# Retention: masked queries made by VectorE from the transposes' PSUM and a state without zero blocks; mLSTM's first masked queries issued first

## The chip, the cores and the metric

The kernel runs on one core of one Trainium2 chip. The metric is the device time of one execution in microseconds (us); the median of three runs counts.

## The reference, cut to what matters

A two-layer streaming encoder works on a prompt of 1024 frames and on eight streams of 16 frames, with a model width of 1024. Each layer normalises its input, multiplies it by one wide input projection, splits the result among four recurrent mixers (mLSTM, retention, SSD, HGRN2), gates each mixer's output, and brings the concatenation back through an output projection. The two mixers that matter here, per chunk of frames and per head (retention has four heads, with a query and key width of 64 and a value width of 128):

```python
# retention_block: carry S (k x v), fixed decay per head
s = einsum("lk,sk->ls", q, k) * dec
o = einsum("ls,sv->lv", s, v) + exp((idx + 1) * lg) * einsum("lk,kv->lv", q, s_prev)
s_new = exp(l * lg) * s_prev + einsum("sk,sv->kv", kw, v)
...
# mlstm_block: carry C (k x v), n, m
s = einsum("lk,sk->ls", q, k) * exp(d - m_t)
num = einsum("ls,sv->lv", s, v) + wi * einsum("lk,kv->lv", q, c_prev)
```

The SSD mixer begins with a causal convolution over four frames (`causal_dwconv`), whose first three input rows of the prompt are zero. All results are float32.

## The kernel before

The 1152 frames (1024 of the prompt, 128 of the eight streams) are nine chunks of 128; chunk 8 is the streams. **Projections** run on TensorE (PE) slab by slab, 256 columns of the weight matrix at a time (`slab_run`, L404 to L406 and L425 to L427). Each weight and activation is split into a high and a low part, so that a float32 product is three passes; ScalarE (ACT) makes the high part of the next slab and VectorE (DVE) or GpSimd (POOL) the low part (`slab_split`). An evacuation function `ev` takes each finished PSUM tile to SBUF.

**The order of the work** is written out by hand. A layer has ten units, `ORDER` = h0, r0, s0, m0, h1, r1, s1, m1, h2, h3 (h is HGRN2, r retention, s SSD, m mLSTM; each r, s and m unit has two heads or one group). `merge` lays the mixing of one unit, a generator `mix` of about 29 steps, between the projection matmuls of the next one: retention is mixed while SSD's projections run, mLSTM while HGRN2's run. So there are four retention units and four mLSTM units in the two layers. Every engine executes its own instructions strictly in the order in which this program issues them, and waits on semaphores for the others. SP issues the DMAs.

**Tiles** come from pools with a fixed number of slots: `t` (9 slots of 256 columns), `f` (18 of 384), `c` (21 of 516), and one PSUM pool of eight tiles for everything (`ps`). A new tile waits until a slot's last reader is done.

**Retention's mix** (L1018 to L1143) treats two heads at once: rows 0 to 63 of a transposed query tile are head 0, rows 64 to 127 head 1. `Z(c)` transposes queries and keys on PE (L1034), and ACT copies both to a `t` tile (L1036). `by_head` (L719) makes the masked ("padded") queries on POOL: two copies of the query tile, each multiplied by `self.HM`, which is 1 on one head's rows and 0 on the other's (L722, printed as the helper's line L212, `t<-t,cst`). `A(c)` multiplies keys by the masked queries (L1045, 256 columns for both heads) and DVE applies the causal mask. `B(c)` adds, in PSUM, the state's part (L1059: queries times `S`, 256 columns) and the scores' part (L1061), and updates the state: L1068, then one DVE addition per head and one scaling of all of `S` (L1077). `S` is 128 x 2 x 128: head 0's block has rows 0 to 63 of the first half, head 1's rows 64 to 127 of the second half, and the other two blocks are zero from a memset (L1020). `Cc(c)` transposes the normalised output (L1113). The steps go A(0); A(1), B(0); A(2), B(1), Cc(0); and so on. Masked queries of chunk c + 1 are asked for right behind A(c), the transposes of chunk c + 2 behind those:

```python
A(c)
if c + 1 < NCH:
    qz[c + 1] = self.by_head(qkT[c + 1][:, 0:128])
if c + 2 < NCH:
    Z(c + 2)
yield
```

**mLSTM's mix** (L770 to L970) has the same masked queries: its `Z(c)` calls `by_head` on the projected queries `q[g]`, and `A(c)` uses them in L833, behind a transpose of the keys (L832). Its first step begins with `load_e(0)`, `load_wi(0)` (DMAs), `use_wi(0)` (a DVE copy L205 `s<-f`, then a POOL product `f<-f,f`), `Z(0)`, `E(0)`.

**SSD's convolution** (`conv` in `unit_s`) copies each projected tile behind three columns of history into a `c` tile; for the first group of frames (g = 0) those three are set to zero by POOL (L1179). DVE then adds three taps (L1197), and SiLU follows on ACT and POOL. The convolution's results `post` and its SiLU's scratch are `f` tiles.

Of the kernel before, what the change touches and what calls it, by code (L numbers as in the profile page):

```python
# [48 lines left out]
NCH = 9  # L49
# [71 lines left out]
class Kernel:  # L121
    def __init__(self, nc, tc, ctx, T):
        self.nc, self.tc, self.T = nc, tc, T
        pool = lambda name, bufs, **k: ctx.enter_context(tc.tile_pool(name=name, bufs=bufs, **k))
        self.p_const = pool("const", 1)
        self.p_big = pool("big", 6)
        self.p_hi = pool("whi", 2)
        self.p_lo = pool("wlo", 2)
        self.p_raw = pool("wraw", 4)
        self.p_f = pool("f", 18)  # L130
        self.p_c = pool("c", 21)
        self.p_t = pool("t", 9)
        self.p_lay = pool("lay", 1)
        self.p_st = pool("st", 1)
        self.p_s = pool("s", 6)
        self.p_bl = pool("bl", 7)
        self.p_dram = pool("dram", 1, space=DRAM)
        self.p_tr = pool("tr", 8, space=PSUM)
        self.n = 0
        self.ticks = 0  # L140
        self.queue = []
        self.steps = 0
        self.after_queue = []
        self.rest = ((), 0)
# [586 lines left out]
    def unit_m(self, l, p):  # L731
# [38 lines left out]
        def mix():  # L770
# [156 lines left out]
            def Cc(c):  # L927
# [12 lines left out]
                if c == 8:  # L940
# [4 lines left out]
                    self.dma(T["o_s_n"][l, :, 2 * p:2 * p + 2].rearrange("n h k -> n (h k)"), nr[0:8])  # L945

            load_e(0)
            load_wi(0)
            use_wi(0)
            Z(0)  # L950
            E(0)
# [30 lines left out]
    def unit_r(self, l, p):  # L982
# [35 lines left out]
        def mix():  # L1018
            S = self.p_st.tile([128, 2, 128], F32, tag="st", name=self.nm("rS"))
            nc.gpsimd.memset(S, 0.0)  # L1020
            qkT, Pt, om, mx, stt, U, qz = {}, {}, {}, {}, {}, {}, {}
            gl = self.cst[:, C_GL:C_GL + 4]
# [6 lines left out]

            def Z(c):  # L1030
                j, i = divmod(c, 2)
                tr = self.ps("tr")
                for a in range(2):
                    nc.tensor.transpose(tr[:, 128 * a:128 * a + 128], qk[j][:, 256 * i + 128 * a:256 * i + 128 * a + 128], self.ident)  # L1034
                t = self.t(256)
                self.copy(t, tr[:, 0:256], "a")  # L1036
                qkT[c] = t
                if c == 8:
                    U["zq"] = [self.zq(t[:, 0:128], slice(64 * h, 64 * h + 64)) for h in range(2)]
                    U["km"] = self.km(qk[j][:, 256 * i + 128:256 * i + 256], "c")  # L1040

            def A(c):
                sc = self.ps("sc")[:, 0:256]
                w = self.t(256).rearrange("p (h t) -> p h t", h=2)
                nc.tensor.matmul(sc, qkT[c][:, 128:256], qz.pop(c), start=True, stop=True)  # L1045
                self.tt(w, sc.rearrange("p (h t) -> p h t", h=2), self.U[c == 8][:, None, :].to_broadcast([128, 2, 128]), ALU.mult)
                Pt[c] = w

            def B(c):
# [5 lines left out]
                if c == 8:  # L1055
                    po[1] = self.ps("sc")[:, 0:128]
                    zq = U.pop("zq")
                if 0 < c < 8:
                    nc.tensor.matmul(pb[:, 0:256], qt[:, 0:128], S.rearrange("p h e -> p (h e)"), start=True, stop=False)  # L1059
                for h in range(2):  # L1060
                    nc.tensor.matmul(po[h], w[:, h], v[j][:, i, h], start=(c in (0, 8)), stop=(c == 0 or (c < 8 and h == 1)))  # L1061
                if c == 8:
# [3 lines left out]
                if c < 8:  # L1066
# [3 lines left out]
                    for h in range(2):  # L1070
                        hs = slice(64 * h, 64 * h + 64)
                        new = tr[hs, 128 * h:128 * h + 128]
                        if c == 0:
                            self.copy(S[hs, h], new, "v")
                        else:
                            self.tt(S[hs, h], S[hs, h], new, ALU.add)
                    nc.vector.tensor_scalar(out=S, in0=S, scalar1=g_, scalar2=None, op0=ALU.mult)  # L1077
                    if c == 7:
                        for h in range(2):
                            self.dma(T["o_p_r"][l, 2 * p + h], S[64 * h:64 * h + 64, h])  # L1080
                else:
# [40 lines left out]
            yield  # L1122
            qz[0] = self.by_head(qkT[0][:, 0:128])
            Z(1)
            yield
            for c in range(NCH + 1):
                if c == 5:
                    load_states()
                if c < NCH:
                    A(c)  # L1130
                    if c + 1 < NCH:
                        qz[c + 1] = self.by_head(qkT[c + 1][:, 0:128])
                    if c + 2 < NCH:
# [14 lines left out]
    def unit_s(self, l, u):  # L1148
# [22 lines left out]
        def conv(a, g, ps):  # L1171
# [5 lines left out]
            e = "av"[(a + g) % 2]  # L1177
            if g == 0:
                nc.gpsimd.memset(t[:, 0:3], 0.0)  # L1179
            else:  # L1180
                self.copy(t[:, 0:3], pre.pop((a, g - 1))[:, 384:387], "v")
# [8 lines left out]
            cb = self.vA[:, 64 + 8 * l + ct:64 + 8 * l + ct + 1]  # L1190
            areas = [(o[:, 0:np_], lambda w: t[:, w:w + np_])]
            if g == 2:
                areas.append((o[:, 256:384].rearrange("p (n t) -> p n t", t=16), lambda w: sv[:, :, w:w + 16]))

            def taps(w):
                for oo, src in areas:
                    nc.vector.scalar_tensor_tensor(out=oo, in0=src(w), scalar=cw(w), in1=oo, op0=ALU.mult, op1=ALU.add)  # L1197

# [823 lines left out]
```

## Time and profile before

| what | us |
|---|---|
| median of three runs | 2413.29 |
| lowest and highest run | 2411.71, 2414.96 |
| the profiled execution | 2415.16 |
| its span, from the first to the last instruction | 2413.4 |

The profiled execution's own time is 1.8 us longer than its span, for what lies around the instructions. The profile lists each instruction with its line, its engine, the tiles that it writes and reads (`out<-in`), its start in us from the span's start, and the idle time of its engine before it with what ended that. PE is the matmul, PEld the weight load that overlaps it. A float32 product that isn't split beforehand appears as two MATMUL records, called passes here. Ends of matmuls are modelled, so the text takes times from start to start. PEclk is the granted TensorE clock as a share of 2.4 GHz.

### The profile page before, as it was taken

Reading aid. Unit: us, or ns where it says so; the run is one execution under the profiler, and the core shown is the slowest. Engines: PE = TensorE matmul, PEld = TensorE weight load, DVE = VectorE, ACT = ScalarE, POOL = GpSimd, SP = SyncE. Lnnn points to the kernel's source line nnn. Section 1 sums busy time; section 2 is a strip of 40 time slices with the busy share of each in tenths; the row PEclk is TensorE's granted clock in tenths of the full one; section 3 lists DMA queues with packets and bytes.
Section 4 is the critical chain, followed back from the end, with each engine's and each line's share of the span. In section 5 each row is a group of like instructions: output and inputs, shape, how many; then the busy total and the mean of one; then the engine's idle time right before and its main releaser. Section 6 shows DMA issues by size and latency. Waiting matters only on the chain.

```text
span 2413.4 us, 49607 instructions
## 1 busy us (share of the span) xinstructions
PE 2333.9 (97%) x18992; PEld 2258.8 (94%) x18992; DVE 1390.7 (58%) x3419; ACT 1076.4 (45%) x2780; POOL 976.2 (40%) x1179
## 2 busy tenths in 40 slices
PE   7999999999999998999989999999999999999998
PEld 7999999999999998899988999999899999888998
DVE  4756753773765376544368376537737654666443
ACT  6344563434455345433243445634344653454332
POOL 2443344353334335423135334432633452345353
PEclk9999999999999999999989999999999999999999
DMA  5111233221123222536411212323111333225552
GB/s 151 37 49 45 81 91 77 65 60 52 50 83 95 61 72 74 158 114 213 133 37 37 61 54 80 90 65 77 49 48 55 98 78 81 50 85 167 159 170 82
DMA packets 273736, 204.06 MB, mean 85 GB/s; under 512 B 57908, under 2 KB 264140, under 8 KB 273500
## 3 DMA queue, kind: packets, MB, share of 16 engines
q1 hardware_dynamic: 273180, 200.81, 29.2%
q8 instruction: 150, 2.46, 0.4%
q14 instruction: 86, 0.70, 0.1%
q0 software_dynamic: 320, 0.09, 0.0%
HBM read 148.53 MB, written 52.29 MB: 83 GB/s over the span
## 4 chain that ended last, share of the span: by engine, by line
PE 83%; DVE 8%; ACT 3%; issue 2%; DMA 1%; POOL 1%; SPq 1%; DVEq 0%; ACTq 0%; POOLq 0%
PE w L425 11%; PE w L404 11%; PE w L427 11%; PE w L426 11%; PE w L406 11%; PE w L405 11%; DVE f L212 3%; ACT f L215 2%; PE w L1310 1%; SPq L218 1%; DVE c L212 1%; PE w L1624 1%; PE w L1663 1%; PE w L1061 1%; PE w L833 1%
## 5 line engine op out<-in xcount | busy, mean ns | idle before, releaser
L425 PE MATMUL w<-hi,hnh 128*128 128x256 f32 (+1 forms) x2592 | 775.8, 299 | 0.0
L427 PE MATMUL w<-hi,hnl 128*128 128x256 f32 (+1 forms) x2592 | 731.9, 282 | 1.6 <-DVE hnl L492 1.6
L426 PE MATMUL w<-lo,hnh 128*128 128x256 f32 (+1 forms) x2592 | 731.7, 282 | 0.1
L425 PEld LDWEIGHTS w<-hi,hnh 128*128 128x128 f32 x2592 | 493.0, 190 | 6.1 <-issue 1.1
L426 PEld LDWEIGHTS w<-lo,hnh 128*128 128x128 f32 x2592 | 493.1, 190 | 3.5 <-issue 0.3
L427 PEld LDWEIGHTS w<-hi,hnl 128*128 128x128 f32 x2592 | 492.5, 190 | 2.2 <-DVE hnl L492 2.0
L215 ACT ACTIVATE f<-f 128x384 f32<-128x384 f32 (+1 forms) x475 | 244.1, 516 | 434.8 <-DVE f L212 275.0
L215 ACT ACTIVATE c<-c 128x512 f32<-128x512 f32 (+3 forms) x398 | 211.3, 534 | 292.4 <-DVE c L546 205.4
L212 POOL TENSOR_TENSOR f<-f,f 128x384 f32<-128x384 f32 (+2 forms) x268 | 226.7, 854 | 283.3 <-ACT f L215 210.3
L404 PE MATMUL w<-hnh,hi 128*128 128x384 f32 x960 | 339.3, 353 | 0.0
L212 POOL TENSOR_TENSOR lo<-raw,hi 128x512 fp32r<-128x512 f32 x148 | 195.0, 1318 | 332.3 <-ACT hi L202 279.2
L406 PE MATMUL w<-hnh,lo 128*128 128x384 f32 x960 | 324.6, 338 | 0.0
L405 PE MATMUL w<-hnl,hi 128*128 128x384 f32 x960 | 324.3, 338 | 0.0
L404 PE MATMUL w<-mxh,hi 128*128 128x384 f32 x768 | 268.7, 350 | 0.0
L406 PE MATMUL w<-mxh,lo 128*128 128x384 f32 x768 | 261.1, 340 | 0.0
L405 PE MATMUL w<-mxl,hi 128*128 128x384 f32 x768 | 260.9, 340 | 0.0
L212 POOL TENSOR_TENSOR c<-c,c 128x512 f32<-128x512 f32 (+2 forms) x120 | 128.9, 1083 | 221.2 <-ACT c L215 175.6
L212 DVE TENSOR_TENSOR lo<-raw,hi 128x512 fp32r<-128x512 f32 x140 | 114.4, 817 | 134.4 <-ACT hi L202 134.2
L404 PEld LDWEIGHTS w<-hnh,hi 128*128 128x128 f32 x960 | 181.6, 189 | 3.0 <-issue 1.8
L405 PEld LDWEIGHTS w<-hnl,hi 128*128 128x128 f32 x960 | 181.8, 189 | 0.8
L406 PEld LDWEIGHTS w<-hnh,lo 128*128 128x128 f32 x960 | 181.0, 189 | 0.0
L212 DVE TENSOR_TENSOR c<-c,w 128x384 f32<-128x384 f32 (+1 forms) x124 | 73.3, 595 | 184.8 <-PE w L406 121.6
(304 smaller groups left out, 3979.3 us busy)
## 6 DMA issues: line engine op xcount, KB each, us to landing
raw<-in_w_in SPq DMA_DIRECT2D x224, 128.0 KB
raw<-in_w_in SPq DMA_DIRECT2D x112, 256.0 KB
c<-mixd SPq DMA_DIRECT2D x96, 192.0 KB
raw<-in_w_out SPq DMA_DIRECT2D x64, 256.0 KB
xd<-c SPq DMA_DIRECT2D x66, 192.0 KB
mixd<-c SPq DMA_DIRECT2D x48, 256.0 KB
c<-xd SPq DMA_DIRECT2D x60, 192.0 KB
c<-sscr SPq DMA_DIRECT2D x36, 256.0 KB
```

Source lines behind the costliest of these rows:

```text
L212: (self.nc.vector if e == "v" else self.nc.gpsimd).tensor_tensor(out=out, in0=a, in1=b, op=op)
L215: self.nc.scalar.activation(out=out, in_=in_, func=func, scale=scale, bias=bias, **k)
L218: (e or self.nc.sync).dma_start(out=out, in_=in_)
L404: nc.tensor.matmul(o, hi[:, k, ms], xhi[:, k, :], start=(k == 0), stop=False)
L405: nc.tensor.matmul(o, hi[:, k, ms], xlo[:, k, :], start=False, stop=False)
L406: nc.tensor.matmul(o, lo[:, k, ms], xhi[:, k, :], start=False, stop=(k == KT - 1))
L425: nc.tensor.matmul(o, xhi[:, k, ts], hi[:, k, :w], start=(k == 0), stop=False)
L426: nc.tensor.matmul(o, xhi[:, k, ts], lo[:, k, :w], start=False, stop=False)
L427: nc.tensor.matmul(o, xlo[:, k, ts], hi[:, k, :w], start=False, stop=(k == KT - 1))
L833: nc.tensor.matmul(sc[:, 0:256], k[g][:, cs], qz.pop(c), start=True, stop=True)
L1061: nc.tensor.matmul(po[h], w[:, h], v[j][:, i, h], start=(c in (0, 8)), stop=(c == 0 or (c < 8 and h == 1)))
L1310: nc.tensor.matmul(po[:, 64 * h:64 * h + 64], pt[:, h], x_[:, 64 * h:64 * h + 64], start=True, stop=True)
```

## The change

Retention's `Z(c)` no longer copies the transposed queries: DVE multiplies them by `HM` straight out of PSUM into the first 256 columns of an `f` tile, and ACT copies the keys, 128 columns, into the last third of it. `by_head` is no longer called by retention; the masked queries of chunk c are thus made in `Z(c)`, which runs two chunks ahead. The state `S` becomes 128 x 128 with both heads' blocks stacked, without zero blocks and memset; `B(c)` multiplies each head's masked queries by all of `S`, two products of 128 columns instead of one of 256. The state's scaling has 128 columns instead of 256. The pool `t` has 8 slots instead of 9. mLSTM's first step calls `Z(0)` ahead of `load_e(0)`. The convolution's first group leaves its three history columns unset and starts each tap at the first column that has a frame behind it.

```diff
@@ -129,7 +129,7 @@
         self.p_raw = pool("wraw", 4)
         self.p_f = pool("f", 18)
         self.p_c = pool("c", 21)
-        self.p_t = pool("t", 9)
+        self.p_t = pool("t", 8)
         self.p_lay = pool("lay", 1)
         self.p_st = pool("st", 1)
         self.p_s = pool("s", 6)
@@ -944,10 +944,10 @@
                     self.copy(nr[0:8], tr[0:8, 0:128], "v")
                     self.dma(T["o_s_n"][l, :, 2 * p:2 * p + 2].rearrange("n h k -> n (h k)"), nr[0:8])
 
+            Z(0)
             load_e(0)
             load_wi(0)
             use_wi(0)
-            Z(0)
             E(0)
             yield
             for c in range(NCH + 1):
@@ -1016,9 +1016,8 @@
             G[c // 2] = z
 
         def mix():
-            S = self.p_st.tile([128, 2, 128], F32, tag="st", name=self.nm("rS"))
-            nc.gpsimd.memset(S, 0.0)
-            qkT, Pt, om, mx, stt, U, qz = {}, {}, {}, {}, {}, {}, {}
+            S = self.p_st.tile([128, 128], F32, tag="st", name=self.nm("rS"))
+            qkT, Pt, om, mx, stt, U = {}, {}, {}, {}, {}, {}
             gl = self.cst[:, C_GL:C_GL + 4]
 
             def load_states():
@@ -1028,21 +1027,24 @@
                     stt[j] = t
 
             def Z(c):
                 j, i = divmod(c, 2)
                 tr = self.ps("tr")
                 for a in range(2):
                     nc.tensor.transpose(tr[:, 128 * a:128 * a + 128], qk[j][:, 256 * i + 128 * a:256 * i + 128 * a + 128], self.ident)
-                t = self.t(256)
-                self.copy(t, tr[:, 0:256], "a")
+                t = self.f()
+                self.tt(t[:, 0:256].rearrange("p (h t) -> p h t", h=2), tr[:, None, 0:128].to_broadcast([128, 2, 128]),
+                        self.HM[:, :, None].to_broadcast([128, 2, 128]), ALU.mult)
+                self.copy(t[:, 256:384], tr[:, 128:256], "a")
                 qkT[c] = t
                 if c == 8:
-                    U["zq"] = [self.zq(t[:, 0:128], slice(64 * h, 64 * h + 64)) for h in range(2)]
+                    U["zq"] = [self.zq(t[:, 128 * h:128 * h + 128], slice(64 * h, 64 * h + 64)) for h in range(2)]
                     U["km"] = self.km(qk[j][:, 256 * i + 128:256 * i + 256], "c")
 
             def A(c):
                 sc = self.ps("sc")[:, 0:256]
                 w = self.t(256).rearrange("p (h t) -> p h t", h=2)
-                nc.tensor.matmul(sc, qkT[c][:, 128:256], qz.pop(c), start=True, stop=True)
+                nc.tensor.matmul(sc, qkT[c][:, 256:384], qkT[c][:, 0:256], start=True, stop=True)
                 self.tt(w, sc.rearrange("p (h t) -> p h t", h=2), self.U[c == 8][:, None, :].to_broadcast([128, 2, 128]), ALU.mult)
                 Pt[c] = w
 
@@ -1055,10 +1057,10 @@
                 if c == 8:
                     po[1] = self.ps("sc")[:, 0:128]
                     zq = U.pop("zq")
-                if 0 < c < 8:
-                    nc.tensor.matmul(pb[:, 0:256], qt[:, 0:128], S.rearrange("p h e -> p (h e)"), start=True, stop=False)
                 for h in range(2):
-                    nc.tensor.matmul(po[h], w[:, h], v[j][:, i, h], start=(c in (0, 8)), stop=(c == 0 or (c < 8 and h == 1)))
+                    if 0 < c < 8:
+                        nc.tensor.matmul(po[h], qt[:, 128 * h:128 * h + 128], S, start=True, stop=False)
+                    nc.tensor.matmul(po[h], w[:, h], v[j][:, i, h], start=(c in (0, 8)), stop=(c < 8))
                 if c == 8:
                     for h in range(2):
                         self.streams_in(po[h], zq[h], lambda n: stt[n // 4][:, n % 4], False)
@@ -1071,13 +1073,13 @@
                         hs = slice(64 * h, 64 * h + 64)
                         new = tr[hs, 128 * h:128 * h + 128]
                         if c == 0:
-                            self.copy(S[hs, h], new, "v")
+                            self.copy(S[hs], new, "v")
                         else:
-                            self.tt(S[hs, h], S[hs, h], new, ALU.add)
+                            self.tt(S[hs], S[hs], new, ALU.add)
                     nc.vector.tensor_scalar(out=S, in0=S, scalar1=g_, scalar2=None, op0=ALU.mult)
                     if c == 7:
                         for h in range(2):
-                            self.dma(T["o_p_r"][l, 2 * p + h], S[64 * h:64 * h + 64, h])
+                            self.dma(T["o_p_r"][l, 2 * p + h], S[64 * h:64 * h + 64])
                 else:
                     g_ = gl[:, 2 + p:3 + p]
                     km = U.pop("km")
@@ -1120,7 +1122,6 @@
 
             Z(0)
             yield
-            qz[0] = self.by_head(qkT[0][:, 0:128])
             Z(1)
             yield
             for c in range(NCH + 1):
@@ -1128,8 +1129,6 @@
                     load_states()
                 if c < NCH:
                     A(c)
-                    if c + 1 < NCH:
-                        qz[c + 1] = self.by_head(qkT[c + 1][:, 0:128])
                     if c + 2 < NCH:
                         Z(c + 2)
                     yield
@@ -1175,9 +1174,7 @@
             t = self.c(411)
             pre[a, g] = t
             e = "av"[(a + g) % 2]
-            if g == 0:
-                nc.gpsimd.memset(t[:, 0:3], 0.0)
-            else:
+            if g > 0:
                 self.copy(t[:, 0:3], pre.pop((a, g - 1))[:, 384:387], "v")
             np_ = G3 if g < 2 else 256
             self.copy(t[:, 3:3 + np_], ps[:, 0:np_], e)
@@ -1188,13 +1185,15 @@
             o = self.f()
             cw = lambda w: self.vA[:, 32 * l + 8 * w + ct:32 * l + 8 * w + ct + 1]
             cb = self.vA[:, 64 + 8 * l + ct:64 + 8 * l + ct + 1]
-            areas = [(o[:, 0:np_], lambda w: t[:, w:w + np_])]
+            areas = [((lambda w: o[:, 0:np_]), lambda w: t[:, w:w + np_])]
+            if g == 0:
+                areas = [((lambda w: o[:, 3 - w:np_]), lambda w: t[:, 3:w + np_])]
             if g == 2:
-                areas.append((o[:, 256:384].rearrange("p (n t) -> p n t", t=16), lambda w: sv[:, :, w:w + 16]))
+                areas.append(((lambda w: o[:, 256:384].rearrange("p (n t) -> p n t", t=16)), lambda w: sv[:, :, w:w + 16]))
 
             def taps(w):
                 for oo, src in areas:
-                    nc.vector.scalar_tensor_tensor(out=oo, in0=src(w), scalar=cw(w), in1=oo, op0=ALU.mult, op1=ALU.add)
+                    nc.vector.scalar_tensor_tensor(out=oo(w), in0=src(w), scalar=cw(w), in1=oo(w), op0=ALU.mult, op1=ALU.add)
 
             def silu():
                 s = self.f()
```

## Rows read from the trace of the kernel before

**Rows 1.** The page's head and its part 1, busy us (share) and instructions per engine.

```profile
span 2413.4 us, 49607 instructions
...
PE 2333.9 (97%) x18992; PEld 2258.8 (94%) x18992; DVE 1390.7 (58%) x3419; ACT 1076.4 (45%) x2780; POOL 976.2 (40%) x1179
```

**Rows 2.** Waits of PE, whole span: who <- releaser: us in total, times, longest.

```profile
PE w L1045 <- POOL c L1179: 7.9, 4, 2.0
...
PE w L833 <- POOL t L212: 3.7, 4, 0.9
```

**Rows 3.** Timeline of PE, first unit: start, us, engine, line, operation, tiles, shape, [idle <-releaser].

```profile
196.09 0.34 PE L406 MATMUL w<-hnh,lo 128*128 128x384 f32 x1
...
196.70 0.38 PE L1034 MATMUL w<-cst,c 128*128 128x128 f32 x2
```

**Rows 4.** Timeline of PE, second retention unit, around A(1).

```profile
600.89 0.34 PE L406 MATMUL w<-hnh,lo 128*128 128x384 f32 x1
...
603.19 0.70 PE L1045 MATMUL w<-t,t 128*128 128x256 f32 x2 [1.96 <-POOL c L1179]
603.72 0.38 PE L1034 MATMUL w<-cst,c 128*128 128x128 f32 x2
```

**Rows 5.** Timeline of POOL, second retention unit, before A(1).

```profile
601.57 0.99 POOL L212 TENSOR_TENSOR f<-f,f 128x384 f32<-128x384 f32 x1 [3.21 <-ACT f L215]
602.52 0.61 POOL L212 TENSOR_TENSOR t<-t,cst 128x256 f32<-128x256 f32 x1
```

**Rows 6.** Windows of equal work around A(1): length, busy per engine, PEclk, DMA, GB/s.

```profile
199.88:206.95 7.07, 5.10 (x21) 4.05 (x21) 2.87 (x6) 2.31 (x6) 2.59 (x4) 0.76 0.15 37
600.89:606.41 5.52, 3.56 (x21) 2.87 (x21) 2.86 (x6) 2.31 (x6) 2.58 (x4) 1.00 0.20 48
1391.81:1397.35 5.54, 3.57 (x21) 2.88 (x21) 2.87 (x6) 2.33 (x6) 2.59 (x4) 1.00 0.28 71
1793.58:1800.59 7.01, 5.05 (x22) 4.14 (x21) 3.11 (x6) 2.30 (x6) 2.58 (x4) 0.76 0.14 37
```

**Rows 7.** Timeline of DVE, first retention unit, around Z(0) and Z(1).

```profile
189.73 0.42 DVE L546 TENSOR_SCALAR c<-w 128x256 f32<-128x256 f32 x1 [2.48 <-PE w L427]
195.59 0.62 DVE L1197 SCALAR_TENSOR_TENSOR f<-c,vA,f 128x384 f32<-128x384 f32 x1 [5.44 <-ACT f L215]
```

**Rows 8.** Groups of DVE by form, whole span: count | busy us, mean ns | idle.

```profile
L212 DVE TENSOR_TENSOR t<-w,cst 128x256 f32<-128x256 f32 x36 | 14.9, 414 | 3.8 <-PE w L1045 3.8
```

**Rows 9.** Timeline of PE, first mLSTM unit, around A(0) and A(1).

```profile
420.62 0.28 PE L427 MATMUL w<-hi,hnl 128*128 128x256 f32 x1
...
421.94 0.70 PE L833 MATMUL w<-t,f 128*128 128x256 f32 x2 [0.93 <-POOL t L212]
...
422.60 0.28 PE L426 MATMUL w<-lo,hnh 128*128 128x256 f32 x1
...
423.77 0.29 PE L427 MATMUL w<-hi,hnl 128*128 128x256 f32 x1
...
424.56 0.28 PE L426 MATMUL w<-lo,hnh 128*128 128x256 f32 x1
```

**Rows 10.** Timeline of POOL, first mLSTM unit, before A(0).

```profile
420.23 1.04 POOL L212 TENSOR_TENSOR f<-f,f 128x384 f32<-128x384 f32 x1 [10.61 <-DVE s L205]
421.23 1.80 POOL L212 TENSOR_TENSOR t<-f,cst 128x256 f32<-128x256 f32 x3
```

**Rows 11.** Timeline of ACT: the first mLSTM unit's first query tile.

```profile
398.65 0.49 ACT L202 ACTIVATE f<-w 128x384 f32<-128x384 f32 x1 [2.37 <-PE w L406]
```

**Rows 12.** Timeline of PE, first retention unit, B(1): state's part, scores' part, update.

```profile
215.50 0.59 PE L1059 MATMUL w<-rS,t 128*128 128x256 f32 x2
215.93 0.61 PE L1061 MATMUL w<-c,t 128*128 128x128 f32 x4
216.38 0.60 PE L1068 MATMUL w<-c,c 128*128 128x256 f32 x2
```

**Rows 13.** Waits of DVE, whole span: us in total, times, longest.

```profile
DVE lo L212 <- ACT hi L202: 134.2, 70, 5.1
```

## The prediction, made before the change ran

> **What bounds the kernel now.** First the page's head and its busy times [rows 1]: TensorE (PE) is busy 97% of the span, VectorE (DVE) 58%, ScalarE (ACT) 45%, GpSimd (POOL) 40%. The reader should see that work on the other three engines costs time only where PE waits for it, and that only 2413.4 - 2333.9 = 79.5 us of the span is left in which PE does nothing. So the second view is the list of PE's own waits [rows 2]. Two of its entries are at lines that the change touches: L1045, the score product of retention's A(c), four times 7.9 us in all, and L833, the same product of mLSTM, four times 3.7 us. Both are put down to POOL. Four is the number of retention units and of mLSTM units (two per layer), so each unit pays once. The third view is the timeline, to see what each of these waits costs from one matmul's start to a later one's.
>
> **Retention's wait.** It falls on the second chunk. In A(0) PE goes from the last projection pass before the scores to the transposes behind them in 196.70 - 196.09 = 0.61 us [rows 3]. In A(1), here of the second unit, the same way takes 603.72 - 600.89 = 2.83 us, with 1.96 us of idle time in it [rows 4]. The wait costs 2.22 us. POOL's own timeline tells why [rows 5]: the masked copy of the queries (L722, `t<-t,cst`) stands behind a product of the convolution's SiLU, and that product waited 3.21 us for ACT. The copy then runs from 602.52, and PE starts as it ends. (The wait's label names POOL's next instruction, the memset of L1179.) So PE waits neither for data nor for POOL's throughput, but for the order of POOL's queue.
>
> The four units do the same work behind this wait, so equal stretches can be laid beside each other [rows 6]: 7.07, 5.52, 5.54 and 7.01 us. In the first and the fourth the mean granted clock is 0.76, not 1.00: after the pause PE spent about half of the stretch at 1.2 GHz and only then went back to 2.4 GHz. That costs 1.55 and 1.47 us more. The four waits together: 4 x 2.22 + 1.55 + 1.47 = 11.9 us.
>
> With the change Z(c) makes the masked queries on DVE out of the transposes' PSUM, two chunks ahead, and A(c) waits for DVE and for an ACT copy half as wide. Would these be in time for A(0) and A(1)? DVE's timeline of the first unit [rows 7] has a clamp ending at 190.15, and then nothing for 5.44 us until the convolution's taps begin at 195.59. Z(0) and Z(1) are issued in that gap (PE's steps are some 3 us apart), each needing one product. For its length I take that of DVE's existing 128x256 product out of PSUM with a broadcast constant, 0.414 us [rows 8]; POOL's copy at 0.61 [rows 5] is the other end. Even at 0.61 both are done before 195.59, while A(0) comes at 196.3 and A(1) would come at 200.1. The waits go whole: **-11.9 us**. The new wait, of DVE for the transposes, has the taps queued behind it and behind those the SiLU on ACT and POOL; but A(c)'s mask, just ahead in DVE's queue, waits for the matmul ahead of those transposes anyway, so it adds at most the transposes themselves, two passes of 128 columns at some 0.11 us [rows 12]. What is late next in A(1) would be the PSUM tile of the scores; no row shows PE waiting for one in this stage.
>
> **mLSTM's wait.** It falls on A(0). PE needs 422.60 - 420.62 = 1.98 us from the last projection pass before it to the second pass behind it; in A(1) the same way takes 424.56 - 423.77 = 0.79 us [rows 9]. The wait costs 1.19 us (its idle time is 0.93; the first passes after it are slower). On POOL, `use_wi(0)`'s product started at 420.23, after 10.61 us of idleness that a DVE copy ended; the masked copy is behind it, from 421.23 [rows 10]. Asked for first, the copy needs only q[0]. ACT wrote the first group of the queries at 398.65 [rows 11], and POOL was idle for 10.61 us. So it is made long before PE asks. Behind it in POOL's queue is only `use_wi(0)`, which still starts when DVE lets it, at 420.23, and ends at 421.23; Z(1) then ends about 421.9, and A(1), moved to some 422.8, finds it ready. Z issues no DMA, so SP's queue keeps its order. **4 x 1.19 = -4.8 us.**
>
> **PE's added work.** The state loses its zero blocks, so for chunks 1 to 7 of four units one product of 256 columns becomes two of 128, each with its own weight load: 28 times. Every such product is two passes. Two passes of 256 take 215.93 - 215.50 = 0.43 us, four passes of 128 with four loads 216.38 - 215.93 = 0.45 us [rows 12]. **28 x 0.02 = +0.6 us.** These passes have the shape of the new ones and load as often, so I take no wider bound. The Trainium skill, "TensorE: Matmul & The Clock Gate", section "LDWEIGHTS (loading the stationary operand)", prices a load of 128 columns at about 107 ns, which speaks against the change: the 56 added loads, if nothing hid them, would cost an estimated 6.0 us, and the sum would be -10.7 instead of -16.1. The trace doesn't agree: a pass of 128 takes 0.11 us with its load in it.
>
> **What costs nothing, and under which cover.** DVE gets 36 products, 36 x 0.414 = 14.9 us, 3.7 per unit. Their cover is DVE's 42% of idle time; if it is gone, PE waits for PSUM evacuations. POOL loses 36 masked copies, 16 memsets of the convolution and four of the state; ACT's copies and DVE's scaling of the state halve. Nobody on PE's path waits for these after the first chunks: 0. The first tap columns of the convolution become up to 3 of 384 narrower: 0. The tiles of Z move from the pool t to f (18 tiles; the convolution of x keeps six through this stage, Z needs four), and t goes from nine to eight. No row shows a wait for a t slot on PE. Between nothing and one more wait of mLSTM's size per mLSTM unit, 4.8 us, I take nothing, since t loses its largest user.
>
> **Sum.** -11.9 - 4.8 + 0.6 = -16.1 us. The profiled execution took 2415.16 us (span 2413.4), 1.9 above the median of the runs; it becomes 2399.1, and the median 2413.29 - 16.1 = **2397.2 us**.
>
> **Rivals.**
> (a) The slow clock isn't part of what is saved. It followed two of four equal pauses [rows 6], so in another execution it may follow none: then 4 x 2.22 + 4.8 - 0.6 = 13.1 us go, 2400.2. The Trainium skill, same page, "What's actually happening", has the clock's watch running freely, so that the slow stretch varies between runs; two of four here agrees. Chance 0.12.
> (b) One wait finds a successor. If mLSTM's A(0) then waits as long for its own transposes, -11.9 + 0.6 leaves 2402.0 (chance 0.08). If it is retention's A(1), for a PSUM tile or DVE, -4.8 + 0.6 leaves 2409.1 (chance 0.05). Against both: the rows of DVE and POOL show the producers idle at the time [rows 7, 10].
> (c) Nothing is gained: PE comes early and gives it all back at its next wait on another engine, +0.6, 2413.9. For it: 68 us of waiting remain elsewhere. Against: what those engines do is started by PE's own evacuations and so moves with PE. Chance 0.05.
> (d) Slower: DVE becomes PE's bound. DVE is in order, and in this stage it also splits weights, waiting for ACT's half: 134.2 us in 70 waits, 1.92 each, 5.1 the longest [rows 13]. A Z product behind such a wait holds its PSUM tile. With two DVE splits for each of three slabs, 24 in the four units, all passed on whole to PE: 24 x 1.92 = 46 us, less 16.1, 2443. It decides once DVE comes back later than PE needs one of its eight PSUM tiles. Against: PE doesn't wait for DVE's other evacuations behind the same waits today. Chance 0.04.
> The forecast keeps 0.66.
>
> **Numbers.** About 0.2% (4.8 us) is what a measurement can tell from no change; the bound of faster is 2408.5. Faster: 0.66 + 0.12 + 0.08 = 0.86; same: the second half of (b) and (c), 0.10; slower 0.04. The range takes in the forecast, (a) and the first half of (b), 0.86 together, and the bound of the t slots, 2397.2 + 4.8 = 2402.0. The three runs spread by 3.3 us, so I add that on both sides: 2393.9 to 2405.3, rounded to 2393.5 and 2405.5.
>
> **What would show it.** Right: L1045 and L833 are gone from PE's waits, or below 0.3 us; DVE has 36 products `f<-w,cst` near 0.41 us, POOL no `t<-t,cst`; the state's product (L1059 before) has 112 passes of 128 columns about 0.11 us apart; PE's idle time is about 68 us; no slow clock follows A(1). Wrong: L1045 still waits, now for DVE; or PE waits in the same stages for a tile that DVE should have emptied; or PE's idle time shrinks as forecast and the time doesn't.

## The result and the profile after

| | median, us | runs | lowest to highest |
|---|---|---|---|
| before | 2413.44 | 4 | 2411.71 to 2414.96 |
| changed | 2398.77 | 4 | 2394.35 to 2400.93 |

The ratio is 0.9937 (95% interval 0.992 to 0.9954): faster by 14.7 us where 16.1 were forecast. Run again beside the experiments below, the changed kernel took 2397.25 us. The profiled execution took 2394.35 us with a span of 2392.3; it is the lowest of the four, and the end of this section says what that adds to the difference of the two profiles.

Page, head and part 1, changed kernel (busy us, share, instructions):

```profile
span 2392.3 us, 49680 instructions
...
PE 2324.5 (97%) x19048; PEld 2254.5 (94%) x19048; DVE 1391.3 (58%) x3455; ACT 1073.8 (45%) x2780; POOL 950.5 (40%) x1123
```

Against [rows 1] PE's idle time fell from 79.5 to 2392.3 - 2324.5 = 67.8 us. DVE's busy time hardly grew in this profile, although DVE took over 36 products of 14.9 us; in the profile of the changed kernel run again it was 1395.6 us. What that rests on is told below. PE's waits, changed kernel (who <- releaser: us in total, times, longest):

```profile
PE w L1604 <- DVE f L212: 10.8, 8, 2.4
PE w L269 <- DMA t<-in_hgrn_norm_w: 9.1, 1, 9.1
PE w L1691 <- DVE f L1682: 7.7, 3, 3.1
PE w L510 <- DVE f L212: 7.4, 2, 4.0
PE w L1584 <- POOL f L212: 6.9, 4, 3.2
PE w L1572 <- POOL f L212: 5.0, 5, 1.2
```

Both entries of [rows 2] are gone: A(c)'s score product is now L1047, mLSTM's is still L833, and neither is in the list, which goes on down to waits of 0.2 us. What leads it lies outside the stages touched. PE's timeline, changed kernel, at A(1) of the second retention unit (compare [rows 4]):

```profile
593.59 0.34 PE L406 MATMUL w<-hnh,lo 128*128 128x384 f32 x1
593.76 0.59 PE L1047 MATMUL w<-f 128*128 128x256 f32 x2
594.19 0.38 PE L1034 MATMUL w<-cst,c 128*128 128x128 f32 x2
```

From the last projection pass to the transposes it is 0.60 us now, as in A(0) before [rows 3], where it was 2.83. Windows of the changed kernel over the same passes as [rows 6] (length, busy of PE, PEld, DVE, ACT, POOL, PEclk, DMA share, GB/s):

```profile
197.53:200.84 3.31, 3.31 (x21) 2.93 (x21) 1.48 (x4) 1.81 (x5) 1.01 (x1) 1.00 0.00 0
593.59:596.88 3.29, 3.29 (x22) 2.92 (x21) 1.46 (x4) 1.79 (x5) 1.02 (x1) 1.00 0.00 0
1380.66:1383.95 3.29, 3.29 (x21) 2.92 (x21) 1.47 (x4) 1.80 (x5) 1.02 (x1) 1.00 0.01 2
1779.33:1782.62 3.29, 3.29 (x21) 2.91 (x21) 1.46 (x4) 1.81 (x5) 1.01 (x1) 1.00 0.00 0
```

PE is busy in all of each window and the granted clock is 1.00 in all four. The windows are 3.76, 2.23, 2.25 and 3.72 us shorter, 12.0 together. DVE's timeline, changed kernel, around Z(0) and Z(1) of the first unit (compare [rows 7]):

```profile
188.10 0.42 DVE L212 TENSOR_TENSOR f<-w,cst 128x256 f32<-128x256 f32 x1 [0.32 <-PE w L1034]
190.96 0.42 DVE L212 TENSOR_TENSOR f<-w,cst 128x256 f32<-128x256 f32 x1 [2.44 <-PE w L1034]
193.15 2.90 DVE L1196 SCALAR_TENSOR_TENSOR f<-c,vA,f 128x381 f32<-128x381 f32 x3 [1.76 <-ACT f L215]
```

Both products are done 6 us before A(1) asks at 197.71. mLSTM's first unit, changed kernel, PE and POOL timelines (compare [rows 9, 10]):

```profile
414.59 0.27 PE L832 MATMUL w<-cst,f 128*128 128x128 f32 x1
414.70 0.60 PE L833 MATMUL w<-t,f 128*128 128x256 f32 x2
```

```profile
414.08 1.04 POOL L212 TENSOR_TENSOR f<-f,f 128x384 f32<-128x384 f32 x1 [10.04 <-DVE s L205]
415.08 1.23 POOL L212 TENSOR_TENSOR t<-f,cst 128x256 f32<-128x256 f32 x2
```

`use_wi(0)`'s product (414.08) still waits some 10 us for DVE, but A(0)'s masked queries no longer stand behind it: L833 starts at 414.70 without idle time, while POOL is still in that product.

**Where the rest of the profiled difference is.** Laying each projection pass of the two profiled executions beside the same pass of the other, the changed kernel's lead grows in the touched stages in eight steps, 3.75, 1.18, 2.22, 1.18, 2.23, 1.19, 3.71 and 1.21 us, 16.7 in all. The two executions differ by 20.8 us; the remaining 4 come from stretches that the change doesn't touch, at the start and near 2195 us, where one execution had the lower clock and the other not. The medians' differences (14.7 us and, run again, 16.5) lie near the 16.7, not near the 20.8.

### The profile page after: what moved, and what is told of

Its sections match the earlier page's. It is cut to its first block, busy times and chain, and to the rows that moved or that the text cites. A ratio compares the mean times of both kernels' runs of the same rounds, so it can differ in the third digit from the quotient of the medians.

```text
span 2392.3 us, 49680 instructions
## 1 busy us (share of the span) xinstructions
PE 2324.5 (97%) x19048; PEld 2254.5 (94%) x19048; DVE 1391.3 (58%) x3455; ACT 1073.8 (45%) x2780; POOL 950.5 (40%) x1123
## 4 chain that ended last, share of the span: by engine, by line
PE 86%; DVE 8%; ACT 3%; issue 1%; POOL 1%; DMA 1%; SPq 0%; DVEq 0%; ACTq 0%; POOLq 0%
PE w L404 12%; PE w L405 11%; PE w L406 11%; PE w L425 11%; PE w L427 11%; PE w L426 11%; DVE f L212 3%; ACT f L215 2%; PE w L1309 1%; DVE c L212 1%; PE w L1572 1%; PE w L1662 1%; PE w L1623 1%; PE w L1063 1%; PE w L489 1%
```

## The experiments

| kernel | median, us (runs) | before, us | ratio [95%] |
|---|---|---|---|
| mLSTM's reordering alone | 2407.99 (11) | 2413.93 | 0.9977 [0.9968, 0.9985] |
| lead of two chunks, still on POOL | 2402.48 (5) | 2413.93 | 0.9955 [0.9942, 0.9968] |
| on DVE, one chunk ahead | 2401.84 (5) | 2413.93 | 0.9959 [0.9947, 0.9971] |
| convolution's part alone | 2416.35 (12) | 2413.93 | 1.0009 [1.0, 1.0019] |
| changed kernel again | 2397.25 (6) | 2413.72 | 0.9934 [0.992, 0.9947] |
| compact state alone | 2417.54 (12) | 2413.72 | 1.0016 [1.0007, 1.0026] |
| changed, 3 more DVE products from PSUM | 2425.29 (6) | 2413.72 | 1.0048 [1.0034, 1.0063] |
| changed, HGRN2's keys two steps earlier | 2405.52 (6) | 2413.72 | 0.9965 [0.9951, 0.9978] |
| changed, 3 more DVE products in SBUF | 2408.76 (7) | 2413.99 | 0.9975 [0.9964, 0.9985] |
| changed, HGRN2's keys asked for one step later | 2402.6 (5) | 2413.99 | 0.9953 [0.9939, 0.9966] |
| changed, 1 more DVE product in SBUF | 2396.67 (5) | 2414.18 | 0.9935 [0.9922, 0.9949] |

**The parts one by one.** The kernel before with mLSTM's part only:

```diff
+            Z(0)
             load_e(0)
             load_wi(0)
             use_wi(0)
-            Z(0)
```

> The kernel before with one edit: mLSTM's first step issues its masked queries ahead of the loads. Theory (PE waits for places in POOL's queue): L833 no longer waits for POOL, four times 1.19 us from start to start, so 4.8 us less than the kernel before, ratio 0.998; the four waits of L1045 stay at 7.9 us. Rival (the gain of the change is retention's alone, and mLSTM's first scores then wait as long for their own transposes or a PSUM tile): L833 waits for another engine instead, within 1 us of the kernel before.

It gained 5.9 us. L833's wait is gone, L1045's stands at 7.9 us as before, and the stretch of passes around A(0), 4.49, 4.75, 4.49 and 4.77 us before, is 3.31, 3.57, 3.31 and 3.56: 4.75 in all. That is the term of 4.8.

The kernel before with only the lead (a full-sized state, POOL still the maker):

```diff
 def Z(c):
     ...
+    qz[c] = self.by_head_f(t[:, 0:128])
...
-            qz[0] = self.by_head(qkT[0][:, 0:128])
...
-                    if c + 1 < NCH:
-                        qz[c + 1] = self.by_head(qkT[c + 1][:, 0:128])
```

> The kernel before with one edit: retention's masked queries are asked for two chunks ahead, right behind the transposes' copy, but still made by POOL (into a wider tile pool, so that no slot is short); state, convolution and mLSTM as before. Theory (the order of POOL's queue): the product for chunk 1 now stands ahead of the convolution's SiLU product, L1045's wait is gone, 8.9 us less (four pauses of 2.22) and up to 12 where slow-clock stretches go with them; ratio 0.995 to 0.9965. Rival (POOL is the wrong engine, only DVE with PSUM at hand is quick enough): L1045 still waits for POOL, 6 us or more in total, and the time is within 3 us of the kernel before.

And only the other engine (DVE makes the masked queries from SBUF, one chunk ahead as before):

```diff
-            qz[0] = self.by_head(qkT[0][:, 0:128])
+            qz[0] = self.by_head_v(qkT[0][:, 0:128])
...
-                        qz[c + 1] = self.by_head(qkT[c + 1][:, 0:128])
+                        qz[c + 1] = self.by_head_v(qkT[c + 1][:, 0:128])
```

> The kernel before with one edit: retention's masked queries are made by DVE instead of POOL, but as late as before, one chunk ahead and out of SBUF; state, convolution and mLSTM as before. Theory (the wait comes from POOL's queue standing behind ACT): on DVE the product for chunk 1 stands behind the mask of chunk 0, which ended at 199.16 in the first unit where PE asked at 200.07, so with some 0.5 us of its own it is just in time: L1045's wait is below 0.5 us in each unit, 8 to 12 us less than the kernel before. Rival (the lead of two chunks is what counts, whatever the engine): L1045 still waits 1.5 us or more in each unit, now for DVE, and at most 3 us are gained.

Either one alone removes the whole wait of A(1): its product (here L1053 and L1052) is in neither list of PE's waits. The two gain the same (11.5 and 12.1 us). mLSTM's wait (L833, here L840) stays, with the same line in both:

```profile
PE w L840 <- POOL t L212: 3.7, 4, 0.9
```

So the wait was a place in POOL's queue: asked for earlier in the same queue, or in another queue, the copy is in time. That the change does both isn't needed for the gain.

The convolution's part alone, a memset less on POOL (and the shorter taps that go with it):

```diff
-            if g == 0:
-                nc.gpsimd.memset(t[:, 0:3], 0.0)
-            else:
+            if g > 0:
                 self.copy(t[:, 0:3], pre.pop((a, g - 1))[:, 384:387], "v")
...
```

> The kernel before with one edit: the convolution's first group without its memset of three columns and with taps that start later. The wait list of the kernel before names that memset as what ended L1045's wait. Theory (the label names POOL's next instruction only): no change, within 1.5 us, and L1045 still waits some 7.9 us in four pauses, now under another name. Rival (the label is right, PE waited for the memset): the wait goes and 9 to 12 us with it.

PE's waits, this kernel:

```profile
PE w L1045 <- POOL t L212: 7.8, 4, 2.0
PE w L833 <- POOL t L212: 3.7, 4, 0.9
```

The wait is the same and now carries the name of the masked copy. So in [rows 2] it was put down to the memset only because that came next on POOL. The memset itself was worth nothing to the wait. The time is 2.4 us above the kernel before, which misses the 1.5 us expected; around A(1) nothing is lost (the four stretches of [rows 6] are 25.18 us together in this kernel and 25.14 before), and where the 2.4 us lie isn't shown.

The compact state alone, the masked queries still late on POOL:

```diff
-            S = self.p_st.tile([128, 2, 128], F32, tag="st", name=self.nm("rS"))
-            nc.gpsimd.memset(S, 0.0)
+            S = self.p_st.tile([128, 128], F32, tag="st", name=self.nm("rS"))
...
+                    if 0 < c < 8:
+                        nc.tensor.matmul(po[h], zz[:, 128 * h:128 * h + 128], S, start=True, stop=False)
...
```

> The kernel before with one edit: retention's state without zero blocks, multiplied by the masked queries, which POOL makes as late as before (kept until the state's product, in a wider tile pool). Theory (the state's form only adds 56 passes of 128 columns with hidden loads, 28 x 0.02 us): within 1.5 us of the kernel before, L1045's wait still 7.9 us, and the state's product 0.9 us with the scores' part instead of 0.88. Rival (the added weight loads aren't hidden): 6 us more, ratio 1.0025.

> The changed kernel as it is, once more, as the reference for the two kernels built on it. Theory: 14 to 17 us less than the kernel before, ratio 0.993 to 0.9945; no wait of PE for the masked queries.

The compact state's median is 3.8 us above the kernel before: more than the 0.6 of the sum and outside the 1.5 expected, while the rival's ratio of 1.0025 lies inside the interval. But the rival's added loads would have to show in the stage, and the extra isn't there. Windows from the same projection pass to the same, behind A(1) to the end of the mixing; first the kernel before, then the compact state alone:

```profile
218.04:289.27 71.23, 71.23 (x536) 69.41 (x536) 53.26 (x140) 33.93 (x78) 24.70 (x32) 1.00 0.21 59
620.54:691.38 70.84, 70.84 (x534) 69.05 (x534) 51.77 (x136) 35.27 (x80) 25.84 (x34) 1.00 0.21 59
```

```profile
214.91:286.23 71.32, 71.32 (x549) 69.78 (x549) 52.80 (x140) 34.19 (x78) 24.93 (x32) 1.00 0.20 59
620.62:691.55 70.93, 70.93 (x547) 69.39 (x547) 51.41 (x136) 35.52 (x80) 26.15 (x34) 1.00 0.21 59
```

It is 0.09 us in each of these two units and some 0.4 in all four. Outside the stage the two profiled executions differ by which pauses the lower clock followed, and the clock goes with a part of the rest: the mean granted clock is 0.9883 over the 12 runs of this kernel and 0.9900 over the 17 of the kernel before taken beside them. From run to run of the kernel before, 0.001 less went with 1.0 to 1.6 us more, so that an estimated 2 to 3 of the 3.8 us go with the clock. Why the lower clock came oftener isn't shown.

**Is DVE near to being the bound?** The changed kernel with three more products straight from PSUM in each Z(c), into an unread tile, behind ACT's copy of the keys:

```diff
                 self.copy(t[:, 256:384], tr[:, 128:256], "a")
+                xtra = self.f()
+                for _ in range(3):
+                    self.tt(xtra[:, 0:256].rearrange("p (h t) -> p h t", h=2), tr[:, None, 0:128].to_broadcast([128, 2, 128]),
+                            self.HM[:, :, None].to_broadcast([128, 2, 128]), ALU.mult)
```

> The changed kernel with three more products of the same form for DVE in each of retention's Z(c), into a tile that nobody reads: 36 x 3 x 0.414 = 44.7 us more of DVE work, 11.2 per unit. It leaves nothing out. Theory (DVE is off PE's path there, with 3 us of room or more): within 2.5 us of the changed kernel, ratio to the kernel before 0.993 to 0.995. Rival (DVE is next in line, so the moved product already costs part of the gain): 8 us or more above the changed kernel, with new waits of PE for DVE in retention's stages.

28 us were lost: the theory was wrong, and the rival's side held, with new waits of PE for DVE. But the experiment held two things at once. PE's waits (the first line of the list), DVE's and PE's timelines, this kernel:

```profile
PE w L1034 <- DVE f L212: 13.9, 8, 2.5
```

```profile
248.15 1.34 DVE L212 TENSOR_TENSOR f<-w,cst 128x256 f32<-128x256 f32 x3 [2.78 <-ACT f L202]
...
249.64 0.66 PE L1034 MATMUL w<-cst,c 128*128 128x128 f32 x2 [2.46 <-DVE f L212]
```

The added products waited 2.78 us for ACT's copy, issued ahead of them, of the same PSUM tile, with all of DVE's queue behind them, and PE's next transposes then waited for that tile. To part load from order, the same number of products in place in SBUF, right behind the first one and ahead of ACT's copy (the masked queries times the 0/1 mask again):

```diff
                         self.HM[:, :, None].to_broadcast([128, 2, 128]), ALU.mult)
+                tq = t[:, 0:256].rearrange("p (h t) -> p h t", h=2)
+                for _ in range(3):
+                    self.tt(tq, tq, self.HM[:, :, None].to_broadcast([128, 2, 128]), ALU.mult)
                 self.copy(t[:, 256:384], tr[:, 128:256], "a")
```

> The changed kernel with three more products on DVE for every pair of masked queries in retention (the masked queries times the 0/1 mask again, in place in SBUF, right behind the first product and ahead of ACT's copy; 36 x 3 of them, by the 0.41 to 0.5 us that such a product takes some 45 to 55 us of DVE's time). Theory: the 28 us that three more products from PSUM cost came from the order in which they stood (DVE held until ACT had copied the same PSUM tile, and the tile held until DVE was done), not from DVE's busy time; here no PSUM tile is held and nothing waits for ACT, so the time is within 2.5 us of the changed kernel's 2397 to 2399, a ratio of 0.993 to 0.995 to the kernel before, and no wait of PE for DVE in retention's stages is above 0.5 us in mean. Rival: it is DVE's load itself that binds in retention's stages; then it is at least 8 us slower than the changed kernel (2406 or more), with PE's transposes and state products waiting for DVE.

Ten to twelve us were lost: the theory was wrong and the rival's number right, though not by a wait for DVE. PE's waits, this kernel:

```profile
PE w L1034 <- ACT f L202: 4.0, 4, 1.0
PE w L1065 <- ACT c L202: 4.0, 4, 1.0
```

ACT's timeline before the second of these, first the changed kernel (run again), then this one, and PE's own at the wait:

```profile
230.69 0.28 ACT L202 ACTIVATE f<-w 128x128 f32<-128x128 f32 x1
230.96 1.64 ACT L215 ACTIVATE f<-f 128x384 f32<-128x384 f32 x3
...
234.13 0.37 ACT L202 ACTIVATE c<-w 128x256 f32<-128x256 f32 x1
```

```profile
236.82 1.64 ACT L215 ACTIVATE f<-f 128x384 f32<-128x384 f32 x3 [2.35 <-DVE f L546]
...
239.55 0.36 ACT L202 ACTIVATE c<-w 128x256 f32<-128x256 f32 x1
```

```profile
239.97 0.38 PE L1065 MATMUL w<-rS,f 128*128 128x128 f32 x1 [1.00 <-ACT c L202]
```

PE is 0.94 us later in this kernel at the passes before that wait, but ACT's exponentials are 5.86 us later, because the DVE clamp ahead of them (L546) is. The evacuation `c<-w` stands behind them in ACT's queue, and PE waits for it: DVE's lateness reaches PE by way of ACT. With one product more instead of three (`range(1)`):

> As the kernel with three in-place products more on DVE per pair of masked queries, but with one (36 in all, some 18 us of DVE's time instead of 54). With three, each retention unit lost 2.45 us in two pauses of about 1.2 us, in both of which PE waited for ACT, whose queue stood behind exponentials that waited for a late DVE clamp. Theory: DVE's lateness costs only from the point at which ACT's evacuation comes later than PE needs the tile, and one product more stays below that point: each unit's stretch after A(1) is within 0.1 us of the changed kernel's (71.17, 70.83, 71.26, 70.84 us), no wait of PE for ACT in retention's stages is in the list, and the time is within 2 us of the changed kernel (2396.5 to 2400). Rival: DVE's work costs in proportion from the first product on, because PE is already as near to it as it can be: then each stretch is about 0.8 us longer (a third of 2.45), 3.3 us in all, with the two waits for ACT about a third as long, and the change's own 36 products have cost about as much and hidden that much of its gain.

The windows behind A(1), first unit and the same passes in each, with DVE's busy time as the fourth number of each: the changed kernel, then one, three in place, three from PSUM.

```profile
211.95:283.12 71.17, 71.17 (x548) 69.66 (x548) 52.90 (x145) 34.08 (x78) 21.45 (x25) 1.00 0.21 61
```

```profile
212.69:283.86 71.17, 71.17 (x548) 69.67 (x548) 56.23 (x150) 33.99 (x78) 21.63 (x25) 1.00 0.21 61
```

```profile
213.93:287.60 73.67, 71.67 (x548) 69.66 (x548) 60.29 (x161) 33.85 (x79) 21.95 (x25) 1.00 0.20 57
```

```profile
213.45:291.27 77.82, 73.33 (x548) 70.99 (x548) 59.97 (x163) 35.13 (x81) 21.68 (x25) 0.98 0.18 53
```

One more costs nothing (71.17 us in both, and the other three units agree to 0.01 us): there is a threshold between one and three, not a price per product. Three in place cost 2.5 us per unit, three from PSUM 6.6, with DVE as busy. So of the 28 us, 4 x 2.5 = 10 go with the work, and about 4 x 4.2 = 17 with what else differs when the products read PSUM. In the trace that is above all the order in which ACT and DVE read one tile (L1034's 13.9 us); the added tile from the pool f was not tested apart from it. DVE is 74% busy in this stretch of the changed kernel (52.90 of 71.17); at 79% (56.23 of 71.17) it was still free, at 82% (60.29 of the longer 73.67) not.

**A faster version?** The largest wait left is PE's for HGRN2's products of the keys (L1604, 10.8 us). Two kernels tried to remove it from the changed kernel, one by making the first group's keys' factors two steps earlier, one by asking for them one step later:

```diff
+                if g > 0:
+                    prep_k(g, W)
...
+            prep_k(0, Ws[0])
```

> The changed kernel with the same remedy at PE's longest remaining wait, the transposes of HGRN2's keys (10.8 us in eight waits, the first group's six among them): the first group's key factors are asked for two steps earlier, so that DVE's product is done when PE comes; the query factors stay. Theory (order of the queues): six of the eight waits shrink below 0.5 us, 6 to 10 us less than the changed kernel. Rival (the other engines are full at the start of these units): the wait moves to the level products before (POOL or DVE), and at most 3 us are gained.

```diff
-                    if li == 1:
+                    if li == (1 if g else 2):
                         keys(g, W)
+                    if li == (3 if g else 4):
+                        state(g, W)
                     if li == 3:
-                        state(g, W)
```

> The changed kernel with the first group of an HGRN2 unit asking for its keys' products one step later and for its state's products one step later (nothing else moved). The costliest wait of PE for DVE in the changed kernel is there: 8 waits of 10.8 us in all for DVE's product, of which 6 stand in the first groups. Theory: they are a matter of where the consumer stands in PE's order; asked for later they fall below 0.5 us each, and the kernel is 6 to 10 us faster than the changed one (2388 to 2393, ratio 0.9895 to 0.9915 to the kernel before). Rival: what PE is short of there is the chain of POOL and ACT before the product, and the later step only moves the wait to the next instruction on PE that needs it (an update of the state or the keys' transposes); then at most 3 us are gained and a wait of like size for POOL or ACT stands in the list in its place.

Both removed that wait, and both were slower than the changed kernel, by 8 and 5 us. PE's waits, the early and then the late one:

```profile
PE w L1575 <- POOL f L212: 15.5, 9, 2.6
```

```profile
PE w L1572 <- POOL f L212: 18.1, 9, 4.4
```

This line, the products of HGRN2's levels, had 5.0 us in the changed kernel (4.5 when run again). The wait moved instead of going: for the early keys where the rival had said, for the late ones to another line than the rival's, but again to one that waits for POOL. That explains why nothing was gained, not why 8 and 5 us were lost, which neither rival had forecast. Part 1 of the page, the changed kernel run again, then the early and the late one:

```profile
PE 2325.1 (97%) x19048; PEld 2254.7 (94%) x19048; DVE 1395.6 (58%) x3455; ACT 1074.6 (45%) x2780; POOL 951.4 (40%) x1123
```

```profile
PE 2335.5 (97%) x19048; PEld 2265.6 (94%) x19048; DVE 1393.9 (58%) x3455; ACT 1075.2 (45%) x2780; POOL 950.0 (40%) x1123
```

```profile
PE 2329.1 (97%) x19048; PEld 2259.3 (94%) x19048; DVE 1392.8 (58%) x3455; ACT 1073.3 (45%) x2780; POOL 951.2 (40%) x1123
```

With spans of 2394.7, 2404.0 and 2399.3 us PE idled 69.6, 68.5 and 70.2 us, so its idle time is nearly the same. The same passes took PE 10.4 and 4.0 us longer, at a mean granted clock of 0.987 and 0.990 instead of 0.992: the loss is time at the lower clock. None of the kernels here is shown to beat the changed one (one more product gave 2396.67 us, the changed kernel again 2397.25, well inside their spread).

## Why the prediction was right, point by point

**Retention's wait, -11.9.** The four windows are 12.0 us shorter. Its cause, the place in POOL's queue, is shown twice, by an earlier place and by another queue.

**The slow clock in that term, 3.0 of the 11.9.** It held for the profiled execution, but that it held there is partly luck, for it isn't fixed. Over the four kernels that keep the wait, the mean granted clock after equal pauses (1.96 to 1.98 us) was 0.76 in units 1 and 4 before, in 2, 3 and 4 with mLSTM's part alone, in 2 and 4 with the compact state and in 1 and 4 with the convolution's: 9 of 16. The first two units with mLSTM's part alone, to be laid beside [rows 6], where it is the other way round:

```profile
198.54:204.07 5.53, 3.55 (x21) 2.85 (x21) 2.86 (x6) 2.32 (x6) 2.59 (x4) 1.00 0.18 47
596.88:603.88 7.00, 5.04 (x21) 4.01 (x21) 2.86 (x6) 2.31 (x6) 2.59 (x4) 0.76 0.14 37
```

At that share four pauses cost 9/16 x 4 x 1.5 = 3.4 us in the mean, and rival (a)'s case, that none is followed by it, has a chance of (7/16)^4 = 0.04 if the pauses are independent: the 0.12 was too much. The Trainium skill's rule behind that rival ("TensorE: Matmul & The Clock Gate", "What's actually happening"), that the slow stretch varies from run to run, agrees with these 9 of 16.

**mLSTM's wait, -4.8.** 4.75, and alone 2407.99 us.

**The state's passes, +0.6.** 0.3 to 0.4 (some 0.09 per unit). The 112 passes of 128 columns (L1062) start 0.11 us apart with their loads, so the loads are hidden. The price per load that spoke against the change (the Trainium skill, same page, "LDWEIGHTS (loading the stationary operand)", an estimated 6.0 us) isn't in any of the four units.

**DVE's products at nothing.** The result was right, its reason too loose. The cover was given as DVE's 42% of idle time, a mean over the span; in the stage where the work landed DVE was already 75% busy (53.26 of 71.23 us in the first unit before), and the cover ends between 3.8 and 13.6 us more per unit (15.3 and 54.2 us in the two runs in SBUF, over four units). Most of the DVE time that the products added was saved elsewhere on DVE, but the cover did not depend on that: one more product per chunk added 15.3 us of work, raised DVE's busy time to 1410.9 us and cost nothing. DVE's groups by form (count | busy us, mean ns), state scaling and Z's products, changed kernel, with the scaling of before first:

```profile
L1077 DVE TENSOR_SCALAR rS<-rS,cst 128x256 f32<-128x256 f32 x32 | 16.6, 519 | 1.1
```

```profile
L212 DVE TENSOR_TENSOR f<-w,cst 128x256 f32<-128x256 f32 x36 | 14.9, 413 | 10.9 <-PE w L1034 10.9
L1079 DVE TENSOR_SCALAR rS<-rS,cst 128x128 f32<-128x128 f32 x32 | 11.3, 352 | 1.1
```

The products took 0.413 us, as in [rows 8]. The scaling gave 5.3 of their 14.9 us back; by the same view the mixing's products `t<-t,c` gave 3.0 (37.3 to 34.3) and the taps of the convolution's first two groups 2.5 (69.5 to 67.0). The taps' smaller width isn't the reason: with the convolution's part alone they took 69.7 us. Both shrank also in the kernel that only moved the masked copies from POOL to DVE (to 32.7 and 66.4). Why isn't shown.

**The rivals.** (b) and (c): no successor, no payback; the lead grows in eight steps and stays. (d) named a mechanism that exists, at the wrong distance: with three more products from PSUM Z's products stood behind a wait for ACT with their PSUM tile held, as (d) has it; with three in SBUF DVE's lateness came by way of ACT's evacuations; with one more, neither. The t slots with one less: no wait in the list.

## What to carry to other kernels

Where an engine with spare time holds PE up once per unit, ask what stands ahead of the awaited instruction in its queue: an earlier place in the same queue was worth as much as another engine. Cover for added work is read in the window where it lands, not from the share of the span, and here it ended at a threshold: test it by doubling the work. When two engines read one PSUM tile, ask which of them the program puts first and whose queue then stands behind the other. Where a removed wait comes back at another line, look at the granted clock too: there the loss lay here.

## What the runs showed of the hardware that wasn't expected

Equal pauses of PE of some 2 us were followed by a stretch at 1.2 GHz in 9 of 16 cases and by none in 7; each such stretch cost about 1.5 us (windows of 7.0 us against 5.5). Two instructions that read one PSUM tile, on DVE and on ACT, ran one after the other in the order of the program: 2.78 us of DVE's time went into waiting for ACT's copy of the other half of the tile. That is how this program is built; what the chip would do without that order, no run shows. Moving waits of PE to another line left its idle time as it was (68.5 us against 69.6), and yet the mean granted clock fell from 0.992 to 0.987, which made its busy time 10.4 us longer.
